# A hybrid RWKV-7 decoder on one core: raw fp32 products in the prologue, centring inside a transposition and split block sums in the scan

## The chip, the cores and the metric

The kernel runs on one core of one Trainium2 chip. The metric is the device time of one execution in microseconds (us), lower is better. TensorE (PE) does the matmuls, VectorE (DVE) and ScalarE (ACT) the element-wise work, GpSimd (POOL) a few memsets; SyncE (SP) and ScalarE issue the DMA transfers.

## What is computed

Two decoder layers of width 2048 on 272 positions (16 learned meta tokens and 256 tokens), all in fp32: RMS norm, RWKV-7 time mixing and a SwiGLU feed-forward, then stick-breaking attention and another feed-forward. The change touches the time mixing only:

```python
def _rwkv7_time_mix(h, ...):
    xx = _token_shift(h) - h
    xr, xw, xk, xv, xa, xg = (h + xx * mu[i] for i in range(6))
    r = xr @ w_r
    k = xk @ w_k
    v = xv @ w_v
    w = -softplus(-(dec_w0 + tanh(xw @ dec_w1) @ dec_w2)) - 0.5
    decay = exp(-exp(w))
    a = sigmoid(a_w0 + (xa @ a_w1) @ a_w2)
    g = sigmoid(xg @ g_w1) @ g_w2
    ...
    kk = heads(k * k_k)                     # 32 heads of 64
    kk = kk * rsqrt(maximum(sum(kk * kk, -1), 1e-24))
    k = k * (1.0 + (a - 1.0) * k_a)
    def step(state, inp):                   # over the 272 positions
        sa = einsum('bhvk,bhk->bhv', state, -kk_t)
        state = state * d_t + sa[..., None] * (kk_t * a_t) + v_t[..., None] * k_t
        return state, einsum('bhvk,bhk->bhv', state, r_t)
    _, y = lax.scan(step, s0, ...)
    y = (y - mean(y)) * rsqrt(var(y) + GN_EPS) * gn_w + gn_b
    bonus = sum(rh * kh * r_k, -1) * vh
    return ((y + bonus) * g) @ w_o
```

## The kernel before

Activations lie with channels on the partitions: 16 tiles of 128 channels by T = 272 positions. A product with a weight matrix is a sum of three fp32r matmuls of the high and low parts of both operands (`mm3k`, L187): `whi` is a rounding copy on ScalarE (L172), `wlo` the difference on VectorE (L173), and `hl` the pair of an activation (`split`, L250). A matmul on plain fp32 operands stands in the trace as two instructions, so each "x8" of such a row is four matmuls.

The time mixing has two stages. The **prologue** (L374) loads x on SP's queue (L385), squares it on ScalarE (L394), sums four squares each on VectorE (L398) and over partitions with a matmul of ones (`ss`, L399), makes the reciprocal root (`rstd_of`, `newton`), the normed `hn` (L452), and the mix `xi` for the keys (L429). The first G0 = 3 of 16 key blocks are multiplied together while x comes in (weights split by `presplit`, L407). `key_out` (L461) copies a finished block and adds its squares' head sums to `kq` (L469). The other 13 blocks follow one by one, and after each a generator `rest()` is stepped RSTEP times: it makes the LoRAs of decay and rate (`lr`, L497, raw fp32), the gate LoRA (mix 5 and `g_w1`, by `proj`), and the mixes for v and r. At the end `kq` becomes the inverse key norms `rk`, which are stored to DRAM (`rkd`) and loaded again as `rn` per pair of heads, spread over partitions.

The **scan** runs over 16 pairs of heads in chunks of 64 positions. `pair` (L580) is a generator; `interleave` (L546) starts a pair every STRIDE = 13 ticks and steps all open ones, so about three pairs overlap. Its steps, in order: `zw`, `za` (decay and rate), the projections of v and r (with `proj_steps`, which are the stream of split products that the small fp32 matmuls are set into), `vc` (values centred by a matmul with `cen`, which is the identity minus the head mean), `ba`/`bb` (scores, masked into G), `bonus` and `z0`, `b00`/`b01` (diagonal blocks, sent to DRAM, where 16-step triangular solves `Ts`, `Tt` are put together and come back), `yb`, `zb`, `tb`/`tv` (transpositions of keys and values), `kv`, `wa`, `rm0`/`rm1` (with `Ah`), `cb` (outputs and the state), `vb` (variance), `gp` (gate). PSUM banks come from three rings by name (FRONT, TAIL, the rest).

Within an engine, instructions run in a fixed order that a list scheduler with its own costs writes when the program is built; tile pools decide which buffer must be free first. SP's queue carries nearly all the weights. ScalarE's queue carries the transfers of the triangular solve.

Of the kernel before, what the change touches and what calls it, by code (L numbers as in the profile page):

```python
# [11 lines left out]
F32 = mybir.dt.float32  # L12
# [6 lines left out]
NK = D // 128  # L19
# [25 lines left out]
NSQ = 4  # L45
RSTEP = 7
KR = 8
# [13 lines left out]
def _consts():  # L61
# [14 lines left out]
    put("blk", blk)  # L76
    put("blk64", blk / 64)
# [6 lines left out]
    put("mask3", np.concatenate([incl, strict, incl], 1))  # L84
# [20 lines left out]
    first = pos  # L105
    put("onesD", np.full((128, 128), 1.0 / D))
# [17 lines left out]
class Builder:  # L124
# [141 lines left out]
    def build(self):  # L266
        tc, nc = self.tc, self.nc
        with ExitStack() as ctx:
# [6 lines left out]
            nc.scalar.dma_start(self.vecs, self.a["vecs"])  # L275
            self.dvec = {"hdw0": 0, "ha0": NK, "oka": 2 * NK}
            self.dvec.update({f"om{i}": (3 + i) * NK for i in range(6)})
            self.dv = cp.tile([128, 9 * NK + 4], F32, name="dv")
            b = 9 * NK
            nc.vector.memset(self.dv[:, b:b + 1], RMS_EPS)  # L280
            nc.vector.memset(self.dv[:, b + 1:b + 2], GN_EPS)
            nc.vector.memset(self.dv[:, b + 2:b + 3], 1.0)
            self.eps = self.dv[:, b:b + 1]
            self.gneps = self.dv[:, b + 1:b + 2]
            self.one = self.dv[:, b + 2:b + 3]

            def v16(name):
                i = VEC.index(name) * NK
                return self.vecs[:, i:i + NK]

            for dst, src in (("hdw0", "dec_w0"), ("ha0", "a_w0")):
                o = self.dvec[dst]
                nc.vector.tensor_scalar(self.dv[:, o:o + NK], v16(src), 0.5, None, ALU.mult)
            nc.vector.tensor_scalar(self.dv[:, 2 * NK:3 * NK], v16("k_a"), -1.0, 1.0,
                                    ALU.mult, ALU.add)
            nc.vector.tensor_scalar(self.dv[:, 3 * NK:9 * NK], self.vecs[:, 0:6 * NK], -1.0, 1.0,
                                    ALU.mult, ALU.add)
            nv = len(VEC) * NK
            self.kgain = self.vecs[:, nv:nv + 1]
            self.qgain = self.dv[:, b + 3:b + 4]  # L300
            nc.vector.tensor_scalar(self.qgain, self.vecs[:, nv + 1:nv + 2], 128.0 ** -0.5, None,
                                    ALU.mult)
# [34 lines left out]

    def time_mix(self):
# [4 lines left out]
        self.xs2 = self.hid_ctx.enter_context(tc.tile_pool(name="xs2", bufs=2 * NK))  # L343
        self.kp = self.hid_ctx.enter_context(tc.tile_pool(name="kp", bufs=NK))
# [6 lines left out]
        with ExitStack() as ctx:  # L351
            sp = ctx.enter_context(tc.tile_pool(name="sp", bufs=1))
            self.l2 = ctx.enter_context(tc.tile_pool(name="l2", bufs=2))
            self.dq = nc.scalar
            self.static = []
            self.s2 = []
            zero = sp.tile([128, 5, 65], F32, name="zero", tag="P")
            nc.gpsimd.memset(zero, 0.0)
            for i in range(2):
                st = {}  # L360
                for n, w in (("B0", 64), ("V0", 64), ("SC0", 128)):
                    st[n] = sp.tile([128, w], F32, name=f"{n}_{i}", tag=f"{n}_{i}")
                    nc.gpsimd.memset(st[n], 0.0)
                self.static.append(st)
                z = self.dram.tile([10, 65, 64], F32, name=f"s2_{i}", tag=f"s2_{i}", bufs=1)
                self.dq.dma_start(z.rearrange("s i t -> (s i t)").rearrange("(p x) -> p x", p=128),
                                  zero.rearrange("p a t -> p (a t)"))
                self.s2.append(z)
            self.interleave(lambda p: self.pair(p, sp), STRIDE, self.wo_head())
# [4 lines left out]
    def prologue(self, hid):  # L374
# [3 lines left out]
        with ExitStack() as ctx:  # L378
# [3 lines left out]
            hn = [self.xs2.tile([128, T + 1], F32, name="hn", tag="s") for _ in range(NK)]  # L382
            xx = [self.xs2.tile([128, T], F32, name="xx", tag="s") for _ in range(NK)]
            for k in range(NK):
                nc.sync.dma_start(xx[k], a["xT"][:, k, :])  # L385
# [14 lines left out]
            rstd = self.rstd_of(ss[:, :T])  # L400


            w0 = [[] for _ in range(G0)]
            raws = []
            n = 0

            def presplit(k0):  # L407
                nonlocal raws, n
                if k0 % 8 == 0:
                    raws = []  # L410
                    for m in range(G0):
                        raw = self.wraw.tile([128, 1024], F32, name="raw", tag="raw")
                        nc.sync.dma_start(raw, a["w_k"][m][:, k0 * 128:k0 * 128 + 1024])
                        raws.append(raw)
                for m in range(G0):
                    pool, t = (wx, ("w", "w")) if n < NWX // 2 else (self.whl, ("whi", "wlo"))
                    hi = pool.tile([128, 512], F32R, name="whi", tag=t[0])
                    lo = pool.tile([128, 512], F32R, name="wlo", tag=t[1])
                    n += 1
                    part = raws[m][:, k0 % 8 * 128:k0 % 8 * 128 + 512]  # L420
                    A.copy(hi, part)
                    V.tensor_tensor(lo, part, hi.bitcast(F32), ALU.subtract)
                    for k in range(4):
                        w0[m].append((hi[:, k * 128:k * 128 + 128], lo[:, k * 128:k * 128 + 128]))
# [5 lines left out]

            def mix(i, k, pool):
                x = pt.tile([128, T], F32, name="xi", tag="tmp")
                mixed(i, k, x)
                if pool is not self.xs2:
# [9 lines left out]
                  for m in range(G0)]  # L444
            xk = []
            for k in range(NK):
                if k % 4 == 0:
                    presplit(k)
                if k == 0:
                    nc.sync.dma_start(self.consts, a["consts"][:, :NC1])  # L450
                V.memset(hn[k][:, 0:1], 0.0)
                V.scalar_tensor_tensor(hn[k][:, 1:], xx[k], self.vec("g_mix0", k), rstd, ALU.mult,  # L452
                                       ALU.mult)
# [5 lines left out]
            self.k = []  # L459

            def key_out(m, ps):  # L461
# [4 lines left out]
                s2 = pt.tile([128, T], F32, name="s2", tag="tmp")  # L466
                A.activation(s2, kt, AF.Square, scale=self.vec("k_k", m))
                o, _ = CONST["sel"]
                nc.tensor.matmul(kq[:, :T], self.consts[:, o + 30 - 2 * m:o + 62 - 2 * m], s2,  # L469
                                 start=m == 0, stop=m == NK - 1)  # L470
# [16 lines left out]
            def rest():  # L487

                for i, name in ((1, "dec_w1"), (4, "a_w1")):
                    ps = self.psd.tile([128, 512], F32, name="lr", tag="sd")[:96, :T]  # L490
                    for k in range(NK):
                        if k % 4 == 0:
                            raw = wx.tile([128, 384], F32, name="raw", tag="w")
                            nc.sync.dma_start(raw, a[name][:, k * 96:k * 96 + 384])
                        x = self.xs1.tile([128, 2 * T], F32, name="xi", tag="hl")[:, :T]
                        mixed(i, k, x)
                        nc.tensor.matmul(ps, raw[:, k % 4 * 96:k % 4 * 96 + 96], x,  # L497
                                         start=k == 0, stop=k == NK - 1)
                        yield 1
                    t = pt.tile([128, T], F32, name=name, tag="tmp")[:96]  # L500
                    if i == 1:
                        A.activation(t, ps, AF.Tanh)
                        self.hw = hsplit(t, name)
                    else:
                        A.copy(t, ps)
                        self.ha = hsplit(t, name)
                for k in range(KR):
                    self.xr.append(mix(0, k, self.xs2))
                    yield 1
                x = []  # L510
                for k in range(NK):
                    x.append(mix(5, k, self.xs1))
                    yield 1
                for j in range(2):
                    ps = self.proj(a["g_w1"][j], x)
                    g = pt.tile([128, T], F32, name="hg", tag="tmp")
                    A.activation(g, ps, AF.Tanh, scale=0.5)
                    V.tensor_scalar(g, g, 0.5, 0.5, ALU.mult, ALU.add)
                    self.hg.append(hsplit(g, f"hg{j}"))
                    yield 1  # L520
# [3 lines left out]
                for k in range(KR, NK):  # L524
# [11 lines left out]
            self.rk = hid.tile([32, T], F32, name="rk")  # L536
# [664 lines left out]
```

## Time and profile before

| | us |
|---|---|
| median of 3 runs (lowest, highest) | 2740.06 (2737.32, 2741.23) |
| profiled execution, its time and its span | 2741.77, 2740.0 |
| first key matmul | 21.2 |
| first `zw` of the scan | 179.8 |
| last `zw` of the scan | 608.3 |
| granted TensorE clock over the span | 0.995 |

The profile is of one execution; its times are us from the start of the span. A row of the timeline is: start, duration, engine, line, operation, output<-inputs, shapes, count, and in brackets the idle time before it with what ended it. Matmuls overlap, so what one costs is the distance between two starts. A row of the chain of waits is start, duration and what ran.

### The profile page before, as it was taken

The numbers are of one execution on the slowest core, as the hardware profiler recorded it, in microseconds if no ns is written. First come the engines' busy times: TensorE is split into PE (matmuls) and PEld (weight loads), VectorE is DVE, ScalarE is ACT, GpSimd is POOL, SyncE is SP. The second block draws the span as 40 slices with busy tenths as digits, with TensorE's granted clock in tenths as the row PEclk, the third lists the DMA queues.
The fourth block names the chain that finished last, engine by engine and source line by source line (L and its number), as shares of the span: only waits on it lengthen the run. The fifth ranks groups of instructions, "written<-read, shape, count | busy, mean of one in ns | idle before, by whom it ended". The sixth has DMA issues, their size and how long they took to land.

```text
span 2740.0 us, 53870 instructions
## 1 busy us (share of the span) xinstructions
PE 2689.3 (98%) x20862; PEld 2475.0 (90%) x20862; DVE 1864.8 (68%) x4176; ACT 1493.5 (55%) x3005; POOL 1.2 (0%) x11
## 2 busy tenths in 40 slices
PE   6999999998999999999999999999999999999999
PEld 5888888887999999999999999988888888888888
DVE  7677788786666555555556876577776666666665
ACT  6774555555554444444445764477555455454553
POOL 0000000000000000000000000000000000000000
PEclk9999999999999999999999999999999999999999
DMA  5443333332655555555555555533555665665655
GB/s 169 135 152 100 104 96 103 104 95 83 210 173 168 181 177 167 185 176 162 187 176 167 180 164 169 169 119 105 189 187 179 196 188 180 197 189 179 199 177 179
DMA packets 181279, 439.50 MB, mean 160 GB/s; under 512 B 57984, under 2 KB 84000, under 8 KB 181024
## 3 DMA queue, kind: packets, MB, share of 16 engines
q1 hardware_dynamic: 137632, 428.56, 49.4%
q10 hardware_dynamic: 43392, 7.52, 1.5%
q8 instruction: 163, 2.67, 0.4%
q14 instruction: 92, 0.75, 0.1%
HBM read 430.27 MB, written 5.74 MB: 159 GB/s over the span
## 4 chain that ended last, share of the span: by engine, by line
PE 91%; DVE 3%; DMA 3%; ACT 2%; ACTq 1%; issue 0%; SPq 0%; DVEq 0%
PE mm L197 22%; PE mm L191 16%; PE mm L193 16%; PE mm L192 15%; PE mm L196 11%; DMA raw<-w_k 1%; PE cb L903 1%; PE yb L831 1%; PE rm L871 1%; PE zb L848 1%; PE hms L1038 1%; PE cb L896 1%; PE z L1115 1%; DVE G L721 0%; PE ba L715 0%
## 5 line engine op out<-in xcount | busy, mean ns | idle before, releaser
L173 DVE TENSOR_TENSOR wlo<-raw,whi 128x512 fp32r<-128x512 f32 (+1 forms) x1596 | 1079.0, 679 | 622.3 <-ACT whi L172 598.7
L172 ACT CAST whi<-raw 128x512 fp32r<-128x512 f32 (+1 forms) x1596 | 967.6, 611 | 906.2 <-PE mm L192 577.0
L191 PE MATMUL mm<-hl,whi 128*128 128x272 f32 x3424 | 996.9, 292 | 19.4 <-ACT hl L254 18.5
L193 PE MATMUL mm<-hl,wlo 128*128 128x272 f32 x3424 | 995.9, 291 | 0.0
L192 PE MATMUL mm<-hl,whi 128*128 128x272 f32 x3424 | 991.4, 290 | 0.4 <-DVE hl L255 0.3
L197 PE MATMUL mm<-hl,whi 128*128 128x512 f32 x2624 | 919.8, 395 | 0.0
L196 PE MATMUL mm<-hl,wlo 128*128 128x256 f32 x2624 | 740.6, 282 | 0.0
L191 PEld LDWEIGHTS mm<-hl,whi 128*128 128x128 f32 x3424 | 645.8, 189 | 27.7 <-ACT hl L254 20.5
L192 PEld LDWEIGHTS mm<-hl,whi 128*128 128x128 f32 x3424 | 652.6, 191 | 4.2 <-DVE hl L255 1.3
L193 PEld LDWEIGHTS mm<-hl,wlo 128*128 128x128 f32 x3424 | 647.9, 189 | 4.8 <-issue 1.8
L197 PEld LDWEIGHTS mm<-hl,whi 128*128 128x128 f32 x2624 | 492.5, 188 | 112.7
L196 PEld LDWEIGHTS mm<-hl,wlo 128*128 128x128 f32 x2624 | 494.3, 188 | 0.6
L213 DVE TENSOR_TENSOR h<-h,mm 128x256 f32<-128x256 f32 (+1 forms) x224 | 93.9, 420 | 6.6 <-PE mm L197 6.0
L206 ACT COPY c<-mm 128x256 f32<-128x256 f32 x104 | 38.8, 373 | 79.0 <-PE mm L197 78.9
L191 PE MATMUL mm<-hi,whi 128*128 128x272 f32 x256 | 79.3, 310 | 0.0
L192 PE MATMUL mm<-lo,whi 128*128 128x272 f32 x256 | 77.0, 301 | 0.0
L193 PE MATMUL mm<-hi,wlo 128*128 128x272 f32 x256 | 76.6, 299 | 0.0
L193 PEld LDWEIGHTS mm<-hi,wlo 128*128 128x128 f32 x256 | 48.8, 191 | 2.9 <-issue 2.4
L191 PEld LDWEIGHTS mm<-hi,whi 128*128 128x128 f32 x256 | 48.9, 191 | 2.4
L192 PEld LDWEIGHTS mm<-lo,whi 128*128 128x128 f32 x256 | 48.9, 191 | 1.0
L428 ACT ACTIVATE u<-hn,vecs 128x272 f32<-128x272 f32 x96 | 45.2, 515 | 4.8 <-DVE hn L452 4.8
L1009 ACT ACTIVATE s<-t 128x272 f32<-128x272 f32 (+1 forms) x88 | 37.5, 426 | 18.6 <-DVE t L208 18.5
(275 smaller groups left out, 2158.6 us busy)
## 6 DMA issues: line engine op xcount, KB each, us to landing
raw<-w_gate SPq DMA_DIRECT2D x176, 512.0 KB
raw<-w_up SPq DMA_DIRECT2D x176, 512.0 KB
raw<-w_down SPq DMA_DIRECT2D x128, 512.0 KB
raw<-w_down SPq DMA_DIRECT2D x128, 192.0 KB
raw<-w_k SPq DMA_DIRECT2D x32, 512.0 KB
raw<-w_v SPq DMA_DIRECT2D x32, 512.0 KB
raw<-w_r SPq DMA_DIRECT2D x32, 512.0 KB
raw<-w_o SPq DMA_DIRECT2D x32, 512.0 KB
```

Of the source, the lines that this page charges most:

```text
L172: nc.scalar.copy(hi, part)
L173: nc.vector.tensor_tensor(lo, part, hi.bitcast(F32), ALU.subtract)
L191: mm(out, w[0], x[0], start=first, stop=False)
L192: mm(out, w[0], x[1], start=False, stop=False)
L193: mm(out, w[1], x[0], start=False, stop=last)
L196: mm(out[:, :n], w[1], x[0], start=first, stop=False, skip_group_check=True)
L197: mm(out, w[0], x[2], start=False, stop=last, skip_group_check=True)
L206: self.nc.scalar.copy(c, out[:, n:])
L213: self.nc.vector.tensor_tensor(h, h, out[:, c:c + n], ALU.add)
L428: A.mul(u, hn[k][:, :T], self.vec(f"mu{i}", k))
L831: PE.matmul(yb[r, i * 64:i * 64 + 64], An[r, i], Tt[r, i], start=True, stop=True)
L1009: nc.scalar.activation(s[:, :n], t[:, :n], AF.Silu)
```

## The change

In the prologue:

- x is loaded on two queues, eight tiles on SP and eight on ScalarE; `vecs` and the constants too are on ScalarE's queue, and the first block of `w_k` is SP's second load. There are 3 buffers for squares instead of 4.
- The rstd chain is one VectorE op shorter: the sign and the factor one half go into the gain `mg0`.
- The three first key blocks are multiplied as raw fp32 (48 matmuls) and not as three split products each (144), so their weights aren't split.
- The gate LoRA is made as the other two LoRAs were, raw fp32 with one mix per channel tile, all three together; `rest()` is stepped 4 times a block and gives xv first, the LoRAs, then xr.
- `kq` is in two halves; the first eight blocks' key norms are stored when block 7 is done.

In the scan:

- `vc` goes. v itself is copied to V0 and ARV, and the centring is done where v is transposed: `z0` with `cen` in the place of the identity, `tv` as eight matmuls of 64 columns, against the identity or `cen`, in the place of four transpositions. The masks take two VectorE ops in the place of four.
- The block sums `bonus` and `vb` are two fp32r matmuls each (high and low part, `head_sums`) with an fp32r block matrix, in the place of one fp32 matmul.
- From VectorE to ScalarE go the copies of `pe`, the affines of `ta` and `k2`, the copy `Ah` and a square; memsets of P go to GpSimd.
- Two pools track reuse of their buffers per tile (`reuse_waits="tile"`).

```diff
-NSQ = 4
-RSTEP = 7
+NSQ = 3
+RSTEP = 4
...
+    def load_tokens(self):
+        for k in range(NK):
+            (nc.sync, nc.scalar)[k % 2].dma_start(self.xx[k], self.a["xT"][:, k, :])
+        nc.scalar.dma_start(self.vecs, self.a["vecs"])
...
-            rstd = self.rstd_of(ss[:, :T])
+            A.activation(r, ms, AF.Ln, bias=self.eps)
+            A.activation(r, r, AF.Exp, scale=-0.5)
+            V.tensor_tensor(rn, r, r, ALU.mult)
+            V.scalar_tensor_tensor(rn, ms, RMS_EPS, rn, ALU.add, ALU.mult)
+            V.scalar_tensor_tensor(rn, rn, -3.0, r, ALU.add, ALU.mult)
...
-                xk.append(mix(2, k, x0))
+                x = xtile()
+                mixed(2, k, x)
                 for m in range(G0):
-                    self.mm3k(ps[m][:, :T], w0[m][k], xk[k], k == 0, k == NK - 1)
-            kq = self.psc.tile([32, 512], F32, name="kq", tag="sc")
+                    o = k % 4 * 128
+                    nc.tensor.matmul(ps[m][:, :T], w0[m, k // 4][:, o:o + 128], x,
+                                     start=k == 0, stop=k == NK - 1)
+                xk.append(self.split(x, x0))
+            kq = [self.psc.tile([32, 512], F32, name="kq", tag="sc") for _ in range(2)]
...
+                if m % 8 < 7:
+                    return
+                ...
+                nc.sync.dma_start(self.rkd[2 * (m - 7):2 * (m + 1)], rk[:16])
...
+                    for i, n in names:        # (1, dec_w1), (4, a_w1), (5, g_w1 twice)
+                        x = xtile()
+                        mixed(i, k, x)
+                        c = 96 if i < 5 else 128
+                        for j in range(len(n)):
+                            nc.tensor.matmul(bk[i, j][:c, :T], w[i, j][:, k % 4 * c:k % 4 * c + c], x,
+                                             start=k == 0, stop=k == NK - 1)
+                    yield 1
...
+        def head_sums(out, block, x, hi):
+            lo = self.rstd_p.tile([128, T], F32R, name="lo", tag="rstdt")
+            V.tensor_tensor(lo, x, hi.bitcast(F32), ALU.subtract)
+            PE.matmul(out, block, hi, start=True, stop=False)
+            PE.matmul(out, block, lo, start=False, stop=True)
...
+        A.copy(V0[:, 32:32 + META], vp[:, :META])
+        A.copy(ARV[:, :, 2], vp[:, META:].rearrange("p (c t) -> p c t", t=C))
...
-        vc = bank("vc")
-        PE.matmul(vc[:, :T], self.cst("cen"), v, start=True, stop=True)
-        A.copy(V0[:, 32:32 + META], vc[:, :META])
-        A.copy(par(ARV, 2, 0), c4(vc[:, :T]))
...
-        PE.matmul(bp[:, :T], self.cst("blk"), rs, start=True, stop=True)
+        head_sums(bp[:, :T], self.blk[0], rs, high(rs))
...
-            PE.matmul(z0[h, 128:192], V0[h], self.cst("eye64")[h], start=True, stop=True)
+            PE.matmul(z0[h, 128:192], V0[h], self.cst("cen")[h, h], start=True, stop=True)
...
-                x = ARV[:, q * 2 + r, 1 - r:3 - r]
-                PE.transpose(tv[:, u:u + 128], x.rearrange("p s t -> p (s t)"), self.cst("ident"))
+                PE.matmul(tv[hs[r], u:u + 128], ARV[:, c, 1], self.cst("ident"), start=True, stop=True)
+                PE.matmul(tv[hs[1 - r], u:u + 128], ARV[:, c, 2], self.cst("cen"), start=True, stop=True)
...
-        V.tensor_copy(Ah, wa.rearrange("p (a s t) -> p a s t", a=4, s=2)[:, :, 0])
+        A.copy(Ah, wa.rearrange("p (a s t) -> p a s t", a=4, s=2)[:, :, 0])
...
-        PE.matmul(vb[:, :T], self.cst("blk64"), sq, start=True, stop=True)
+        head_sums(vb[:, :T], self.blk[1], sq, high(sq))
```

What the scheduler makes of it, at three places. **ScalarE at the start of the program.** A name in brackets is a semaphore waited for; DMAHW1, 3, 5, 7 count the landings of earlier transfers, of which DMAHW3's is the first block of `w_k` (`raw`). Before:

```order
L275 DMA vecs<-vecs 128x290
L387 ACT_TABLE_LOAD
L394 ACTIVATE sq<-xx 128x272 [waits DMAHW1_49]
L394 ACTIVATE sq<-xx 128x272 [waits DMAHW2_49]
L394 ACTIVATE sq<-xx 128x272 [waits DMAHW3_49]
L394 ACTIVATE sq<-xx 128x272 [waits DMAHW4_49]
```

and after:

```order
L317 DMA vecs<-vecs 128x290
L316 DMA xx<-xT 128x272
L413 ACT_TABLE_LOAD
L316 DMA xx<-xT 128x272 x2
L316 DMA xx<-xT 128x272 [waits DMAHW1_49]
L316 DMA xx<-xT 128x272 [waits DMAHW3_49]
L316 DMA xx<-xT 128x272 [waits DMAHW5_49]
L316 DMA xx<-xT 128x272 [waits DMAHW7_49]
L316 DMA xx<-xT 128x272 [waits DMAHW1_49]
L420 ACTIVATE sq<-xx 128x272
L420 ACTIVATE sq<-xx 128x272 [waits DMAHW2_49]
L420 ACTIVATE sq<-xx 128x272 [waits DMAHW4_49]
```

Behind the vecs come eight loads of x (`xx`), five of which wait for an earlier landing, and all stand ahead of the first square (`sq`).

**SP's queue from the last key blocks to the first pairs of the scan.** Before, `rkd` is the store of all the inverse key norms (`rk`), and the first `rn` loads them for pair 0; the `lora` rows are the second LoRA weights, `w_v` and `w_r` the projections of the first pairs. Before:

```order
L161 DMA raw<-w_v 128x1024 x2
L161 DMA raw<-w_r 128x1024 x2
L161 DMA raw<-w_v 128x1024 x2
L614 DMA w_2285<-lora 128x512
L161 DMA raw<-w_r 128x1024
L544 DMA rkd<-rk 32x272
L614 DMA w_2580<-lora 128x512
L161 DMA raw<-w_r 128x1024
L625 DMA rn<-rkd 128x1x272
```

After, in the key blocks,

```order
L541 DMA raw<-a_w 128x384
L160 DMA raw<-w_k 128x1024
L507 DMA rkd<-rk 16x272
L541 DMA raw<-g_w 128x512 x2
L160 DMA raw<-w_k 128x1024 x2
```

and, at the end of the key blocks,

```order
L160 DMA raw<-w_k 128x1024 x7
L160 DMA raw<-w_v 128x1024 x2
L160 DMA raw<-w_r 128x1024 x2
L160 DMA raw<-w_v 128x1024 x2
L657 DMA w_2032<-lora 128x512
L668 DMA rn<-rkd 128x1x272
L507 DMA rkd<-rk 16x272
L657 DMA w_2327<-lora 128x512
```

The store of the first half (pairs 0 to 7) has moved among the key weights, and pair 0's `rn` stands ahead of the store of the second half.

**TensorE in the scan, where values are transposed.** `mm` rows are the stream of split products, the others belong to two pairs under way. Before:

```order
L848 MATMUL zb<-Ys,Tn 64x64 x8
L801 MATMUL tv<-consts,ARV 128x128 x4
L191 MATMUL mm<-hi,whi 128x272
L192 MATMUL mm<-lo,whi 128x272
L857 MATMUL wa<-X,Tt 64x128 x8
L810 MATMUL kv<-X,G 64x64 x8
L695 MATMUL vc<-v,consts 128x272
L871 MATMUL rm_5811<-G,Ah 64x128 x2
L871 MATMUL rm_5812<-G,Ah 64x128 x2
```

After, from the last two of the eight `tv` matmuls on:

```order
L834 MATMUL tv<-consts,ARV 64x128
L835 MATMUL tv<-consts,ARV 64x128
L891 MATMUL wa<-X,Tt 64x128 x8
L844 MATMUL kv<-X,G 64x64 x8
L905 MATMUL rm_6078<-G,Ah 64x128 x4
L190 MATMUL mm<-hi,whi 128x272
L905 MATMUL rm_6079<-G,Ah 64x128 x4
L191 MATMUL mm<-lo,whi 128x272
L192 MATMUL mm<-hi,wlo 128x272
```

`vc` no longer stands between `kv` and the first `rm`, and one product now divides the two `rm` banks. In the same way `b00`, `b01` and `yb`, which were one block of small matmuls, stand at three places, with products between, and the low part of `bonus` stands inside `z0`. A pair has 16 such visits to small matmuls where it had 14.

More of the change, by code (lines that the diff above doesn't have):

```diff
@@ L105, in _consts @@
     first = pos
+    put("blk", blk)
     put("onesD", np.full((128, 128), 1.0 / D))
@@ L274, in build @@
             self.vecs = cp.tile([128, NV], F32, name="vecs")
[L275 to L302, printed above, removed]
+            self.dv = cp.tile([128, 12 * NK + 5], F32, name="dv")
             self.rstd_p = ctx.enter_context(tc.tile_pool(name="rstd", bufs=1))
@@ L366, in time_mix @@
                 self.dq.dma_start(z.rearrange("s i t -> (s i t)").rearrange("(p x) -> p x", p=128),
-                                  zero.rearrange("p a t -> p (a t)"))
+                                  zero)
                 self.s2.append(z)
+            o, n = CONST["blk"]
+            raw = sp.tile([128, 5, 64], F32, name="blk", tag="Tt", bufs=BUFS["Tt"])
+            raw = raw.rearrange("p c t -> p (c t)")[:, :n]
+            self.dq.dma_start(raw, a["consts"][:, o:o + n])
+            self.blk = []
+            for i, x in enumerate((1.0, 1.0 / HD)):
+                t = sp.tile([128, n], F32R, name="blk", tag=f"blk{i}")
+                nc.scalar.activation(t, raw, AF.Copy, scale=x)
+                self.blk.append(t)
             self.interleave(lambda p: self.pair(p, sp), STRIDE, self.wo_head())
@@ L381, in prologue @@
             pt = ctx.enter_context(tc.tile_pool(name="pt", bufs=3))
[L382 to L385, printed above, removed]
+            hn, xx = self.hn, self.xx
             self.pre0 = tc.keep_in_program_order(
@@ L399, in prologue @@
                 nc.tensor.matmul(ss[:, :T], od, acc, start=g == 0, stop=g == NK - 4)
-            rstd = self.rstd_of(ss[:, :T])
[L403 to L424, printed above, removed]
+            ms = ss[:, :T]
+            r = self.rstd_p.tile([128, T], F32, name="rstd", tag="rstd")
+            rn = self.rstd_p.tile([128, T], F32, name="rstdt", tag="rstdt")
+            A.activation(r, ms, AF.Ln, bias=self.eps)
[3 more added lines that the diff above has]
+            V.scalar_tensor_tensor(rn, rn, -3.0, r, ALU.add, ALU.mult)
             def mixed(i, k, out):
@@ L465, in key_out @@
                 self.k.append(kt)
[L466 removed]
+                s2 = xtile()
                 A.activation(s2, kt, AF.Square, scale=self.vec("k_k", m))
                 o, _ = CONST["sel"]
[L469 to L470 removed]
+                o += 30 - 2 * (m % 8)
+                nc.tensor.matmul(kq[m // 8][:, :T], self.consts[:, o:o + 32], s2,
+                                 start=m % 8 == 0, stop=m % 8 == 7)
+                if m % 8 < 7:
+                    return
+                rk = hid.tile([32, T], F32, name="rk", tag="rk")
+                t = self.rstd_p.tile([128, T], F32, name="kqs", tag="rstd")[:32]
+                V.tensor_scalar(t, kq[m // 8][:, :T], 1e-24, None, ALU.max)
+                t2 = self.rstd_p.tile([128, T], F32, name="kqr", tag="rstdt")[:32]
+                A.activation(rk, t, AF.Ln)
+                A.activation(rk, rk, AF.Exp, scale=-0.5)
+                self.newton(rk, t, 0.0, t2)
+                nc.sync.dma_start(self.rkd[2 * (m - 7):2 * (m + 1)], rk[:16])
             for m in range(G0):
@@ L487, in rest @@
             def rest():
[L489 to L520, printed above, removed]
                 for k in range(NK):
@@ L605, in bank, with high @@
             return self.psc.tile([128, 512], F32, name=name, tag="sc")
+        def head_sums(out, block, x, hi):
[3 more added lines that the diff above has]
+            PE.matmul(out, block, lo, start=False, stop=True)
+        def high(x):
+            hi = self.rstd_p.tile([128, T], F32R, name="hi", tag="rstd")
+            A.copy(hi, x)
+            return hi
         def c4(ap):
```

178 lines of the change are left out of this document (119 added, 59 removed).

## The prediction, made before the changed kernel ran

> **What bounds the kernel now.** I read the page first, then the waits of TensorE, then windows over the stages, then the timeline and the chain of waits at the places that the change touches.
>
> ```profile
> span 2740.0 us, 53870 instructions
> PE 2689.3 (98%) x20862; PEld 2475.0 (90%) x20862; DVE 1864.8 (68%) x4176; ACT 1493.5 (55%) x3005; POOL 1.2 (0%) x11
> ```
> ```profile
> PE mm L191 <- ACT hl L254: 18.5, 7, 6.7
> PE b L766 <- DVE bv L729: 5.8, 11, 0.6
> ```
> ```profile
> 21.20:53.40 32.20, 26.41 (x150) 24.16 (x150) 26.99 (x61) 21.21 (x50) 0.00 (x0) 0.90 0.44 138
> 53.40:179.80 126.40, 122.53 (x859) 108.28 (x858) 93.55 (x198) 100.88 (x230) 0.99 (x7) 1.00 0.45 145
> 190.00:195.00 5.00, 2.76 (x26) 2.38 (x26) 4.85 (x16) 0.62 (x1) 0.00 (x0) 0.89 0.37 135
> 195.00:200.00 5.00, 5.00 (x45) 3.80 (x44) 1.82 (x6) 1.44 (x5) 0.00 (x0) 0.77 0.72 228
> 225.00:230.00 5.00, 2.22 (x12) 1.67 (x11) 1.34 (x7) 1.69 (x4) 0.00 (x0) 0.80 0.25 53
> 230.00:235.00 5.00, 5.00 (x46) 4.34 (x45) 3.50 (x12) 0.83 (x2) 0.00 (x0) 0.51 0.33 96
> 300.00:500.00 200.00, 196.37 (x2391) 167.64 (x2390) 160.26 (x577) 115.46 (x277) 0.00 (x0) 1.00 0.36 101
> ```
>
> In the second fence each row gives a waiting instruction, what it waited for, total us, times, longest. In the third it is the stretch and its length, then busy us of PE, PEld, DVE, ACT and POOL, the granted clock, DMA share and GB/s. TensorE is busy 98% of the span, so outside a few waits only its own work counts. The scan (300 to 500) leaves it idle 3.6 of 200 us. VectorE and ScalarE, from which much work is taken, are filled to 80% and 58% there, and what they give back is free time, apart from TensorE's wait for `bv`: 5.8 us in 11 times, 0.53 a pair. The waits that can be won lie in the first 53 us and in the fill of the pipeline (190 to 235), and there an idle is paid twice: the windows behind the two holes run at clocks of 0.77 and 0.51. From the projection `w_o` on, neither the work nor its order changes, so the last 2000 us are costed at nothing.
>
> **The start: x on two queues.**
>
> ```profile
> 3.50 0.97 ACT L394 ACTIVATE sq<-xx 128x272 f32<-128x272 f32 x2 [1.02 <-DMA xx<-xT]
> 12.27 0.43 ACT L394 ACTIVATE sq<-xx 128x272 f32<-128x272 f32 x1 [0.73 <-PE ss L399]
> 13.23 1.28 PE L399 MATMUL ss<-sq,od 128*128 128x272 f32 x2 [1.00 <-DVE sq L398]
> 17.38 0.69 DVE L422 TENSOR_TENSOR wlo<-raw,whi 128x512 fp32r<-128x512 f32 x1 [0.29 <-ACT whi L421]
> 18.79 0.51 DVE L452 SCALAR_TENSOR_TENSOR hn<-xx,vecs,rstd 128x272 f32<-128x272 f32 x1
> 21.23 1.05 PE L191 MATMUL mm<-hl,whi 128*128 128x272 f32 x3 [6.72 <-ACT hl L254]
> ```
> ```profile
> 4.96 0.43 SPq L385
> 8.76 7.95 DMA raw<-w_k
> ```
> ```profile
> 63.64 4.36 DMA raw<-w_k
> ```
>
> Before, ScalarE squares from 3.50, and the last square (12.27) waits not for data but for a `ss` matmul to free a buffer. Afterwards ScalarE's own queue holds vecs and eight x loads (0.43 each) ahead of the first square, and the fifth of them waits until a block of `w_k`, now SP's second load, has landed. Such a block takes between 4.36 us (row at 63.64) and 7.95 us (row at 8.76), so that one issued at 1.2 lands at 5.6 to 9.2. I take 6.5, near the low end, as one x tile and not sixteen is ahead of it in its queue. Four issues more put the first square at about 8.0, 4.5 us later. Three square buffers instead of four I cost at nothing, because the pace is already that of the sums; uncovered, each group of four would wait one `ss` matmul, 1.28 us. With the same 9.7 us from first square to last `ss` matmul, that one starts at 17.7 against 13.23. From there to the first key matmul it is 8.0 us before. The splits of weights among the VectorE steps go (the 0.69 at 17.38 and another ahead of the first split of x), so do one op of the rstd chain and the split of x ahead of the matmul; behind `hn` stand only u and xi, three steps of about 0.5. I take 5.6. The key matmuls start at 23.3 instead of 21.2: **+2.1**, between −2.4 (no wait in the queue) and +4.8 (7.95 holds).
>
> The Trainium skill (DMA: Bandwidth & Descriptors, Issuing engines are not separate DMA queues) says that transfers started from several engines run on the same 16 DMA engines, and only the issuing time is saved. The trace agrees as far as it goes, since the issuing (0.43 a tile) isn't what the last square waits for; by that rule alone this part would be worth nothing rather than +2.1.
>
> **Three key blocks raw.**
>
> ```profile
> 60.73 0.29 PE L193 MATMUL mm<-hl,wlo 128*128 128x272 f32 x1
> 60.85 2.00 PE L497 MATMUL lr<-xi,raw 128*96 128x272 f32 x8
> 62.78 0.65 PE L469 MATMUL kq<-s,consts 128*32 128x272 f32 x2
> ```
>
> A split product starts 0.12 us after the one before; eight fp32 passes, which are four fp32 matmuls, take 1.93 us, 0.24 a pass. 144 products (18 us) become 48 raw matmuls (96 passes, 23.0 us). The stretch from 21.2 to 53.4 is 32.2 us long though, TensorE idle for 5.8 of it and at a clock of 0.90: it waits for `hl` and weight splits. Twelve pairs of weight splits go, x is split only for later blocks, and the loads of the second half no longer wait for a buffer. So the stage becomes TensorE's: 23.0, plus 2.6 lost to the clock (0.10 of 32.2 is 3.2 before, some of it behind later holes), plus 1.0 where VectorE doesn't keep up: 26.6 to the first key sum, **−5.6**. The cover there is thin: VectorE needs hn, xi and a split per k, three steps of 0.4 to 0.5, against six passes, 1.44. If it falls behind throughout, 2 us more go.
>
> The Trainium skill (TensorE: Matmul & The Clock Gate, Part 1: The HAM clock gate) puts the slow time at about 3.4 us of activity. At half pace that loses 1.7 us; the 3.2 us that this stretch lost is more, and the holes in it are why I don't go lower. By the page the stage would come out 0.9 us shorter.
>
> **Gate LoRA raw.** Its 96 split products (11.8 us) become 32 raw matmuls (64 passes, 15.4): +3.6. In the stretch from 53.4 to 179.8 TensorE idles 3.9 us, and with fewer splits for VectorE and ScalarE I take 2.1 of that back: **+1.5** (between −0.3 and +3.6). The LoRAs' new places and the smaller step of the generator only reorder work on a TensorE that is full. The pipeline's first `zw` (179.8 now) comes 2.0 us earlier.
>
> **The fill.**
>
> ```profile
> 183.45 6.67 DMA rn<-rkd
> 192.84 0.37 PE ba L715
> 222.34 6.27 DMA Tt<-s
> ```
>
> The chain of waits goes from the last key block through `rk`, its store and its load (6.67 us) to `ba` of pair 0, for which TensorE idles 2.24 us (190 to 195) and then loses 0.11 and 0.23 of 5 us each to the clock, 1.7: 3.9. With `kq` in two halves the first half's store stands ahead of all of that on SP's queue, and pair 0's `rn` waits for eight key blocks only. What is late next is the triangular solve of pair 0: `Tt` returns from DRAM at 228.6, an idle of 2.78 us (225 to 230), and the clock costs 1.0 and 2.45 more: 6.2. Its chain has the same links but starts with `rn`; I take a third, 2.1, and keep 0 and 6.2 as bounds. **−6.0**.
>
> **The scan, per pair.**
>
> ```profile
> 437.73 0.66 PE L801 MATMUL tv<-consts,ARV 128*128 128x128 f32 x4
> 438.14 0.37 PE L191 MATMUL mm<-hi,whi 128*128 128x272 f32 x1
> ...
> 439.68 0.73 PE L695 MATMUL vc<-v,consts 128*128 128x272 f32 x2
> 440.33 1.30 PE L871 MATMUL rm<-G,Ah 64*64 64x128 f32 x16
> ```
> ```profile
> 438.00 0.40 ACT L661 COPY v<-mm 128x272 f32<-128x272 f32 x1
> 438.42 0.59 ACT L802 COPY X<-tv 128x512 f32<-128x512 f32 x1
> ```
> ```profile
> 439.70 0.43 DVE L861 COPY Ah<-wa 128x256 f32<-128x256 f32 x1
> ```
> ```profile
> 449.36 0.29 PE L192 MATMUL mm<-hl,whi 128*128 128x272 f32 x1
> 449.58 0.33 PE L903 MATMUL cb<-Rh,S 64*64 64x64 f32 x4
> ...
> 450.07 0.29 PE L191 MATMUL mm<-hl,whi 128*128 128x272 f32 x1
> ...
> 450.44 0.69 PE L916 MATMUL vb<-sq,consts 128*128 128x272 f32 x2
> ...
> 451.18 0.37 PE L715 MATMUL ba<-ARV,BK 64*128 64x128 f32 x1
> ...
> 453.62 0.69 PE L727 MATMUL bonus<-rs,consts 128*128 128x272 f32 x2
> 454.24 0.30 PE L734 MATMUL z<-AR,B 64*64 64x32 f32 x4
> ```
>
> Starts are what counts. `vc` occupies 0.65 (439.68 to 440.33) and goes: −0.65. `bonus` occupies 0.62; two split products take 0.25, but the second stands inside `z0` and cuts it in two. A visit from the stream of split products to small fp32 matmuls costs about 0.3 by itself: 0.71 from 449.36 to 450.07, less two products and some 0.16 of small passes. So bonus is −0.07. `vb` with the `gp` product behind it occupies 0.74, afterwards three products, 0.38: −0.36. `tv` was 0.41 for four transpositions; eight matmuls of half the columns, if two of them run side by side, are sixteen passes of 128 columns in eight slots, about twice the work and a switch: +0.55. `b00`, `b01` and `yb`, one visit now, become three: +0.6. In exchange `b00` waits only for ScalarE's copy and `b01` for `bv`, with split products between: −0.53, the wait in the fence of waits. `Ah` moves to ScalarE, queued there behind the copies of X (0.59), v (0.40) and V0, and `rm0` needs it at once; `vc` had filled that gap of 0.65. I take half of it: +0.35. Other moves of copies and affines from VectorE to ScalarE are hidden under TensorE's 98%; if ScalarE were late, the whole pair stands behind it. The sum is −0.1 a pair, **−1.6** over 16. Ends: −0.45 a pair (no wait for `Ah`), −7; +0.95 (`rm0` waits for all three copies, 1.42), +15. At the tail the chain to the last output changes a copy of 0.4 for a shorter rstd: 0.
>
> **The sum.** +2.1 − 5.6 + 1.5 − 6.0 − 1.6 = −9.6. The profiled execution took 2741.77 (span 2740.0 and 1.8 around it), 1.7 above the median of 2740.06; 2741.77 − 9.6 is 2732.2, on the median's scale 2730.5, so **2731**.
>
> **Rivals.**
> - ScalarE's queue becomes what TensorE waits for in the scan: `rm0` stands until X, v and `Ah` are copied, 1.42 a pair. At +0.95 a pair the scan gains 15 us, against −8.0 before it: 2747. It ends as slower from +0.85 a pair on, and eats the gain from +0.5. For it: TensorE has no slack there, and the filler `vc` is gone; `tv` at two slots for one (+0.5 to +0.8) would do the same. Against it: ScalarE is filled to only 58%. Chance 0.22.
> - The early gain is taken by the next wait: `Tt` comes as late as before and idles longer, the squares start at 10.7. Then −9.6 + 2.7 + 2.1 + 1 of clock: −3.8, 2736, no measurable change. For it: each hole shown is followed by another one in the chain. Chance 0.25.
> - The whole of it works: squares hardly delayed (−2), `Tt`'s hole closed too (−4), the scan at −0.45 a pair (−5): 2719. For it: holes cost double by the clock, and each closed one returns that. Chance 0.13.
> - My forecast, 2722 to 2735: chance 0.40.
>
> Under 0.2% (5.5 us) the measurement of this kernel can't tell a difference from none. Faster: nearly all of the forecast and the third rival, 0.50; within: 0.27, the second rival and the forecast's edge; slower: 0.23. The range reaches from 2715 (the third rival, with its clock regained too) to 2749 (the first, 2 beyond its price).
>
> **What would show it.** First square near 8 and key matmuls near 23; the first `kq` near 50; no hole ahead of the first `ba`, one of about 2 us ahead of `yb`; no wait for `bv` in the scan, and successive pairs as far apart as now, to 0.2 us. I'm wrong if the pairs stand over 0.5 us further apart, if `rm0` shows a wait for `Ah` of over half a us a pair, or if ScalarE's squares start at 4 or past 10.

## The result, and the profile after

The changed kernel takes 2750.32 us (median of 5 runs, 2748.74 to 2752.61) against 2738.69 for the kernel before on the same chip (5 runs): 1.0042 times as long, 95% interval 1.0028 to 1.0057. It is slower by about 11.6 us; the prediction was 2731, and its range ended at 2749. Of the two profiled executions the one before took 2741.77 and the one after 2748.74, so that the traces show 7.0 us of the 11.6 between them; the rest is the spread of runs.

First the marks that the prediction named. The start, in the timeline of the changed kernel:

```profile
1.69 6.92 ACTq L316 DMA_DIRECT2D xx<-xT  x7
8.65 0.75 ACT L420 ACTIVATE sq<-xx 128x272 f32<-128x272 f32 x2 [5.71 <-DMA xx<-xT]
...
18.69 1.27 PE L425 MATMUL ss<-sq,od 128*128 128x272 f32 x2 [1.54 <-DVE sq L424]
24.21 6.09 PE L477 MATMUL mm<-xi,raw 128*128 128x272 f32 x13 [4.24 <-DVE xi L439]
```

ScalarE is busy with issuing x until 8.6, and squares from 8.65 (3.50 before). The key matmuls start at 24.2 (21.2 before). Windows of the changed kernel, columns as in the prediction: the raw key blocks, the other key blocks, the two stretches that held the holes of the fill, and eight pairs of the steady scan. Behind them, in a second fence, the same eight pairs before.

```profile
24.20:51.30 27.10, 25.63 (x98) 20.38 (x98) 23.01 (x53) 18.67 (x45) 0.00 (x0) 1.00 0.35 116
51.30:181.30 130.00, 125.69 (x832) 109.41 (x832) 82.87 (x176) 92.08 (x206) 1.06 (x9) 1.00 0.44 139
190.00:195.00 5.00, 4.64 (x66) 3.53 (x65) 4.38 (x10) 3.31 (x8) 0.14 (x2) 1.00 0.55 161
225.00:230.00 5.00, 5.00 (x75) 4.25 (x74) 4.86 (x20) 3.21 (x8) 0.00 (x0) 1.00 0.06 18
344.40:583.40 239.00, 237.70 (x2883) 203.95 (x2884) 175.29 (x602) 151.33 (x384) 1.09 (x16) 1.00 0.35 99
```
```profile
344.20:577.30 233.10, 228.96 (x2804) 195.47 (x2801) 187.64 (x681) 133.52 (x321) 0.00 (x0) 1.00 0.36 102
```

The holes ahead of `ba` and `yb` are gone but for 0.36 us, and with them the half pace: the clock is 1.00 in both stretches. But a steady pair takes 239.0/8 = 29.87 us instead of 29.14. Per pair TensorE idles 0.16 us instead of 0.52, and is busy 1.09 longer (237.70 against 228.96, over eight). VectorE got 12 us lighter over these pairs and ScalarE 18 heavier; neither decides anything here. Three of the waits of TensorE in the changed kernel (us in total, times, longest) show that `bv` has left the list and little has come in its place.

```profile
PE yb L865 <- DMA Tt<-s: 1.9, 2, 1.5
PE bonus L642 <- DVE G L755: 1.4, 4, 0.4
...
PE rm L905 <- ACT Ah L895: 0.4, 1, 0.4
```

What the busy time is made of. From the starts of all matmuls of those eight pairs I summed the distance from each start to the next by the tile written; us per pair:

| tile | before | after | |
|---|---|---|---|
| vc | 0.66 | 0 | −0.66 |
| tv | 0.41 | 1.02 | +0.61 |
| wa, kv, rm | 2.34 | 2.74 | +0.41 |
| bonus | 0.62 | 0.48 | −0.15 |
| vb, gp | 1.47 | 1.12 | −0.35 |
| z0 | 0.50 | 0.74 | +0.25 |
| b00 and b01 | 0.29 | 0.77 | +0.48 |
| mm (before it holds the wait of 0.52 ahead of b) | 14.75 | 14.85 | +0.10 |

The remaining tiles make +0.04. The step from a product into a visit to small matmuls stands in the row of the product (mm), the step out of it in the row of its last small pass. In the timeline of TensorE the cuts can be seen (`b` is b00 in one row and b01 in the other):

```profile
381.89 0.98 PE L891 MATMUL wa<-X,Tt 64*64 64x128 f32 x14
382.65 0.27 PE L844 MATMUL kv<-X,G 64*64 64x64 f32 x2
...
383.45 0.66 PE L905 MATMUL rm<-G,Ah 64*64 64x128 f32 x8
...
394.77 0.28 PE L770 MATMUL z<-consts,V 64*64 64x64 f32 x2
394.98 0.39 PE L643 MATMUL bonus<-lo,blk 128*128 128x272 f32 x1
395.30 0.32 PE L770 MATMUL z<-consts,V 64*64 64x64 f32 x2
...
397.26 0.46 PE L798 MATMUL b<-BK,ARV 64*64 64x64 f32 x8
400.34 0.46 PE L798 MATMUL b<-BK,ARV 64*64 64x64 f32 x8
```

In the timeline before, one row held all sixteen b passes:

```profile
458.53 0.48 PE L766 MATMUL b<-BK,ARV 64*64 64x64 f32 x16 [0.52 <-DVE bv L729]
```

Start to end that took 0.48, behind the wait for `bv`; now two rows of eight take 0.46 each, three us apart.

### The profile page after: what moved, and what is told of

Its sections match the earlier page's. It is cut to its first block, busy times and chain, and to the rows that moved or that the text cites. A ratio compares the mean times of both kernels' runs of the same rounds, so it can differ in the third digit from the quotient of the medians.

```text
span 2747.0 us, 54045 instructions
## 1 busy us (share of the span) xinstructions
PE 2702.8 (98%) x20942; PEld 2483.8 (90%) x20942; DVE 1826.2 (66%) x3988; ACT 1515.9 (55%) x3101; POOL 3.3 (0%) x43
## 4 chain that ended last, share of the span: by engine, by line
PE 95%; DMA 2%; DVE 1%; ACT 1%; issue 0%; ACTq 0%; DVEq 0%; SPq 0%
PE mm L196 22%; PE mm L190 16%; PE mm L192 16%; PE mm L191 16%; PE mm L195 11%; PE lr L547 1%; PE yb L865 1%; DMA raw<-w_k 1%; PE cb L937 1%; PE rm L905 1%; PE zb L882 1%; PE hms L1074 1%; PE wa L891 1%; PE cb L930 1%; PE z L1151 1%; PE mm L477 0%
## 5 line engine op out<-in xcount | busy, mean ns | idle before, releaser
L190 PE MATMUL mm<-hl,whi 128*128 128x272 f32 x3344 | 972.6, 291 | 8.4 <-ACT hl L253 5.6
L192 PE MATMUL mm<-hl,wlo 128*128 128x272 f32 x3344 | 969.7, 290 | 0.0
L191 PE MATMUL mm<-hl,whi 128*128 128x272 f32 x3344 | 967.8, 289 | 0.0
L190 PEld LDWEIGHTS mm<-hl,whi 128*128 128x128 f32 x3344 | 629.8, 188 | 16.2 <-ACT hl L253 5.9
L191 PEld LDWEIGHTS mm<-hl,whi 128*128 128x128 f32 x3344 | 636.0, 190 | 3.0 <-issue 0.5
L192 PEld LDWEIGHTS mm<-hl,wlo 128*128 128x128 f32 x3344 | 630.5, 189 | 3.6 <-issue 1.5
L196 PEld LDWEIGHTS mm<-hl,whi 128*128 128x128 f32 x2624 | 492.5, 188 | 111.5
L195 PEld LDWEIGHTS mm<-hl,wlo 128*128 128x128 f32 x2624 | 493.9, 188 | 0.6
```

The source lines that it names most:

```text
L190: mm(out, w[0], x[0], start=first, stop=False)
L191: mm(out, w[0], x[1], start=False, stop=False)
L192: mm(out, w[1], x[0], start=False, stop=last)
L195: mm(out[:, :n], w[1], x[0], start=first, stop=False, skip_group_check=True)
L196: mm(out, w[0], x[2], start=False, stop=last, skip_group_check=True)
```

## Experiments

Theory A: the change is slower because the order that comes with it cuts the small matmuls of a pair into more and less overlapping pieces, and because ScalarE's queue holds up the start; the new prologue by itself gains. Rival B: the new operations (`tv`, the split sums) are dearer in themselves. Rival C: ScalarE's copies are what TensorE waits for. In all texts "visit" is an entry from the stream of split products into small fp32 matmuls. Every ratio is against the kernel before on the same chip. The changed kernel's own interval, 1.0028 to 1.0057, overlaps those of experiments 2, 3, 4 and 5, so that between these and it the windows decide and not the times. A pass is one of the two instructions of an fp32 matmul.

**1 and 2. The scan of before; x on SP's queue.** The first takes back the whole `pair` generator, the second one line.

```diff
-            (nc.sync, nc.scalar)[k % 2].dma_start(self.xx[k], ...)
+            nc.sync.dma_start(self.xx[k], ...)
```

> The changed prologue with the pair generator of before (vc, four transpositions, single fp32 block sums, Ah on VectorE). Theory A (the scan as it is ordered now costs TensorE 0.7 us a pair more): pairs again 29.1 us apart, first zw near 181.4 as in the changed kernel, the fill keeps its gain; 2733 to 2738 us. Rival B (the prologue costs it): pairs matter little, the time stays above 2745.

> All sixteen x loads back on SP's queue, everything else as changed. Theory A (the squares wait for ScalarE's own issues): first square near 3.5 instead of 8.65, key matmuls near 20.5 instead of 24.2, first zw 3 to 4 us earlier, 2747 us. Rival (x is limited by the transfers themselves, the queue doesn't matter): key matmuls at 23.5 or later, no change of the time.

Experiment 1: 2738.32 us, ratio 0.9996 (0.9986 to 1.0006). Its first `zw` comes at 181.8, its sixth at 310.5, its last at 603.4; its pairs are 29.1 apart. So the scan carries the slowdown. What prologue and fill gained together stays inside the noise of the runs; in the trace the last `zw` is 4.9 us ahead of before, where the prediction had 8.0. Experiment 2: 2746.62, ratio 1.0029 (1.0017 to 1.0040). Its timeline:

```profile
3.54 0.43 ACT L420 ACTIVATE sq<-xx 128x272 f32<-128x272 f32 x1 [1.08 <-DMA xx<-xT]
...
16.54 0.49 ACT L430 ACTIVATE rstd<-ss,dv 128x272 f32<-128x272 f32 x1 [2.07 <-PE ss L425]
```
```profile
20.74 9.59 PE L477 MATMUL mm<-xi,raw 128*128 128x272 f32 x29 [4.24 <-DMA raw<-w_k]
```

Squares from 3.54 and key matmuls from 20.7, as expected: the second queue cost 3.5 us at this place, of which 2.5 are left at the first `zw` (178.9 against 181.4; 3 to 4 were expected). The key matmuls now wait last for a block of `w_k`, which stands behind all of x on SP's queue.

**3, 4 and 6. Order only.** The matmuls of `z0` are pinned behind the low product of `bonus` (3); also `yb` begins with the half that lands last (4); or those of `b00` and `b01` are chained in turn (6).

```diff
+            self.tc.keep_in_program_order(   # each z0 matmul (3, 4)
             PE.matmul(z0[h, 0:32], B0[h], ...)
-                for r in hs:                 # first yb (4)
+                for r in hs[::-1]:
+            if n: self.tc.keep_in_program_order(mm)   # b00, b01 (6)
```

> Order only: z0's six matmuls are kept together behind the low product of bonus, so bonus no longer cuts z0 in two; the order has 15 visits to small fp32 matmuls a pair instead of 16. Theory A (each visit costs about 0.35 by itself): pairs 29.5 us apart instead of 29.86, 2745 us. Rival C (what costs is the new work, or waits for ScalarE's copies, wherever it stands): 29.8 to 29.9, or a new wait for lo ahead of z0.

> Order only: as the one before, and yb begins with the half whose transfer is issued last, so that it isn't begun alone; the scheduler then makes an order with 10 to 11 visits a pair instead of 16. Theory A: 0.35 for each visit, so pairs about 27.9 us apart, 2722 us, if no new wait comes up. Rival C: visits are free, the pairs stay at 29.5 to 29.9, 2745 to 2750.

> Order only: the matmuls of b00 and b01 (two row halves of the array, two banks) alternate again but for the first. Theory A (apart, each half has the array alone, and the sixteen passes cost 0.77 where alternating they cost 0.29): b down to about 0.4, pairs 29.5 us apart, 2745 to 2746. Rival: the second bank comes free late, so the chain of b waits and the pairs stay at 29.9.

Medians and ratios: (3) 2745.48, 1.0027 (1.0017 to 1.0036); (4) 2758.85, 1.0071 (1.0054 to 1.0088); (6) 2741.71, 1.0008 (0.9998 to 1.0017). The windows over eight pairs, of 3, then 4, then 6:

```profile
342.80:580.40 237.60, 234.61 (x2883) 201.92 (x2883) 175.24 (x601) 151.22 (x384) 1.10 (x16) 1.00 0.35 100
```
```profile
343.00:591.60 248.60, 231.44 (x2886) 202.17 (x2884) 171.79 (x601) 153.54 (x384) 1.10 (x16) 0.99 0.33 95
```
```profile
342.00:580.00 238.00, 236.70 (x2883) 202.94 (x2882) 175.11 (x601) 151.23 (x384) 1.09 (x16) 1.00 0.34 100
```

(3) went as A said in sign and time: TensorE's busy time fell by 0.39 a pair, of which 0.2 was lost again to b's bank, so a pair took 29.70, not 29.5. (4) missed: the busy time did fall, to 28.93 a pair, but TensorE now idled 2.1 a pair. In (6) a pair gained 0.11 and not the expected 0.36 (29.75), since the first of the eight matmuls of b still stands alone, three us ahead of the other seven:

```profile
394.67 0.32 PE L798 MATMUL b<-BK,ARV 64*64 64x64 f32 x2
...
397.74 0.47 PE L798 MATMUL b<-BK,ARV 64*64 64x64 f32 x14
```

From start to start b fell from 0.77 to 0.65 a pair. So the overlap that came back is worth 0.12, and most of what b costs more than before stays as long as there are two visits. The time came out 3 us below the expected 2745, which A doesn't explain: of the 7.3 us of span, 2.8 came from the first zw to the sixth and 3.9 behind the last one, which no theory named. What (4) waited for, in its waits, in ScalarE's timeline and, third, in the chain of waits:

```profile
PE bonus L642 <- ACT hi L647: 11.1, 8, 3.1
```
```profile
457.72 0.49 ACT L955 ACTIVATE rs<-vb,dv 128x272 f32<-128x272 f32 x1
460.19 1.30 ACTq L818 DMA_DIRECT2D Tt<-s  x2
461.53 1.28 ACT L956 ACT_TABLE_LOAD   x1 [3.32 <-issue]
462.82 0.43 ACT L956 ACTIVATE rs<-rs 128x272 f32<-128x272 f32 x1
```
```profile
455.90 4.27 DMA s<-Ts
```

ScalarE does nothing from 458.2 to 461.5: its next entry is the load of `Tt`, which waits for the store that goes before it (`s<-Ts`, 4.27 us). The copy of bonus's high part stands behind that and a table load.

**5. The block sums as one fp32 matmul each again.**

```diff
-        head_sums(bp[:, :T], self.blk[0], rs, high(rs))
+        PE.matmul(bp[:, :T], self.blk[0], rs, start=True, stop=True)
```

> The changed kernel with bonus and vb as one plain fp32 matmul each, as before; the scheduler's order then has 14 visits a pair and z0 whole, b00 and b01 still apart. Theory A (a visit costs 0.35, the split sums themselves save TensorE about 0.5 a pair): +0.5 for the sums, -0.35 for z0, -0.35 for another visit less, pairs 29.6 to 29.7 us apart, 2747. Rival B (the split sums are what makes a pair dearer): pairs 29.2 or less, 2740.

2754.55, ratio 1.0052 (1.0039 to 1.0066). Both missed: pairs are dearer still, 31.2, of which 1.4 is idle. Rival B falls for the sums. For `tv` no run tests it; there the table has its price, +0.61. The waits name the reason for the idle, b's bank (freed by the copy `BV`), 0.9 each time, and `Tt`:

```profile
PE b L798 <- ACT BV L775: 9.0, 10, 1.3
...
PE yb L865 <- DMA Tt<-s: 3.3, 6, 1.1
```

**7 and 8. The prologue alone, without the second queue; and with the gate LoRA in split products.** 7 is 1 and 2 together; 8 puts back all of `rest()` as before, with its order of mixes and its 7 steps a block.

> Scan of before, changed prologue, all x on SP's queue: the first two experiments together. Theory A (their effects add): key matmuls at 20.7, first zw near 179, pairs 29.1, 2735 us, faster than before by 0.2%. Rival: the earlier start meets weights that have not landed, and 2738 stays.

> As e7, and the gate LoRA as split products again (with the order of the other LoRAs as before). Theory A (raw costs TensorE 3.6 us there and frees no wait): first zw 2 to 3.5 us earlier than in e7, 2732 us. Rival (the splits of mix 5 and g_w1 keep VectorE and ScalarE from the key blocks): no earlier zw, 2735 or more.

7: 2733.40, ratio 0.9979 (0.9970 to 0.9987), faster than both kernels; first `zw` at 177.3, 2.5 ahead of before. 8: 2735.72, 0.9988 (0.9978 to 0.9997). Its first `zw` comes at 175.3, 2.0 earlier than in 7, as A said, but its fourth at 255.7 against 248.5. The holes of the fill are back: from the first `zw` to the sixth TensorE idles 7.2 us at a clock of 0.96, as before. So the time is where the rival had it. Since one edit changed both, the run can't tell which part of the new `rest()` keeps the fill closed. The intervals of 7 and 8 overlap, so which is the better isn't shown.

**9 and 10. The pins together; b apart in the old scan.** 9 is 2, 3 and 6 together. 10 writes the four matmuls of b00 (eight passes) ahead of the four of b01 in experiment 7's kernel, within the same visit:

```diff
-        for c, h in order:
+        for c, h in sorted(order, key=lambda x: x[1]):
```

> The changed kernel with x on SP's queue and the two pins on the order (z0 whole, b00 and b01 alternating). Theory A (the effects add: 3.7 + 4.8 + 8.6 less than the changed kernel): pairs 29.5 to 29.6 us apart, 2734 us. Rival (the pins change the tail or the fill by chance, not the pairs): the sum doesn't come out, 2738 to 2742.

> The scan of before (as e7) with b00's matmuls written ahead of b01's; the order of all else is the same, 14 visits, both behind the wait for bv. Theory A (alternating matmuls of two row halves share the array): b from 0.28 to 0.5 or more a pair, pairs from 29.10 to 29.35 us apart, 2737 us. Rival (what cost in the changed kernel was the second visit alone): b stays at 0.28 to 0.35, 2733 us.

9: 2737.16, 0.9992 (0.9984 to 1.0001). The pairs came out at 29.6, the time 3 us above the sum: the 8.6 of experiment 6 did not add. 10: 2733.80, 0.9979 (0.9970 to 0.9988), pairs of 29.13, b at 0.28 from start to start as in 7.

```profile
450.51 0.48 PE L797 MATMUL b<-BK,ARV 64*64 64x64 f32 x16 [0.53 <-DVE bv L760]
```

A missed here, and the rival was met: the turn of the matmuls within a visit doesn't matter, so what b costs in the changed kernel comes with its second visit.

**11 and 12. The split sums in the old scan; Ah back on VectorE.**

```diff
-        PE.matmul(bp[:, :T], self.blk[0], rs, start=True, stop=True)   # 11, and vb alike
+        head_sums(bp[:, :T], self.blk[0], rs, high(rs))
-        A.copy(Ah, wa...)                                              # 12
+        V.tensor_copy(Ah, wa...)
```

> The scan of before (as e7) with bonus and vb as two split products each, the scheduler then makes an order of 13 to 15 visits. Theory A (the products save 0.35 with vb and 0.15 with bonus, the order they bring decides the rest): pairs 28.6 to 29.6 us apart, with waits for the high part's copy or for b's banks named in the trace; about 2731. Rival B (split sums are a loss by themselves): over 29.6.

> The changed kernel with the copy Ah on VectorE again; the scheduler makes an order of 13 to 16 visits. As predicted blind: rm0's wait for Ah goes, 0.2 to 0.35 a pair less, and fewer visits give another 0.5: pairs 29.2, 2742. Rival (ScalarE's queue in general, not this copy): no less than 29.7, with other waits for ScalarE.

11: 2756.06, 1.0064 (1.0053 to 1.0076), pairs of 31.0, of which 1.3 idle; TensorE is busy 29.7 where it was 28.6 in 7. A missed. The number is rival B's, but the rows of the sums themselves fell against 7 (`vb` with `gp` −0.24, bonus −0.05), while b rose from 0.28 to 0.65. 12: 2760.34, 1.0075 (1.0062 to 1.0088), pairs of 30.9, 1.0 idle. A missed in 12; the rival's bound (no less than 29.7) held, but it hadn't named the size: taking away a wait that stands in the list with 0.4 us cost 10 us, since the order became another one, whose longest waits in the scan are these five:

```profile
PE zb L882 <- DVE Ys L876: 3.1, 4, 1.1
PE bonus L642 <- ACT hi L647: 2.9, 4, 1.2
PE b L798 <- ACT BV L775: 2.7, 3, 1.0
PE yb L865 <- DMA Tt<-s: 2.2, 2, 1.6
PE b L798 <- DVE bv L762: 2.1, 2, 1.8
```

**13 and 14. The high part's copy on VectorE**, in 9's kernel and in 4's (both with x on SP).

```diff
-            A.copy(hi, x)
+            V.tensor_copy(hi, x)
```

> As e9 (new scan, x on SP, z0 whole, b chained), with the copy of the high part of bonus and vb on VectorE instead of ScalarE; the scheduler's order then has 12 visits a pair, the same every pair. Theory D (a visit between split products costs TensorE 0.3, provided the order holds no new wait): three visits fewer and b overlapped once more, 0.9 to 1.3 less than e9's 29.6: pairs 28.3 to 28.7 us apart, 2717 to 2722 us. Rival E (an order with fewer visits packs work that then waits, as in e4 and e12): idle of 0.8 or more a pair, pairs 29.3 or more, 2735 or slower.

> As e4 (z0 and yb whole, which waited 1.3 a pair for the high part's copy of bonus on ScalarE, behind the transfer of the triangular solve), with that copy on VectorE and x on SP; the order has 9 to 13 visits, not the same every pair. Theory E1 (the wait in e4 is for ScalarE's queue): no wait for hi left, idle below 0.6 a pair, pairs 29.0 or less, 2735 or less. Rival E2 (the wait is for rs, which comes late on VectorE, or for the buffer that bonus and vb share): the wait for hi stays at 0.8 or more a pair, above 2745.

13: 2738.48, 1.0000 (0.9990 to 1.0010). 14: 2730.56, 0.9971 (0.9960 to 0.9982): 8 us below before and the fastest by its median, though its interval overlaps those of 7 and 10. Windows over eight pairs, 13, then 14 (whose order differs from pair to pair):

```profile
341.70:576.10 234.40, 229.21 (x2881) 199.52 (x2880) 176.81 (x617) 146.61 (x369) 1.09 (x16) 1.00 0.35 101
```
```profile
337.50:567.40 229.90, 228.19 (x2897) 199.24 (x2897) 175.42 (x616) 145.69 (x368) 1.09 (x16) 1.00 0.36 103
```

14 against 4 bears out theory E1: with the copy off ScalarE's queue, the 11.1 us of waits for it shrink to one of 0.4, and the idle falls from 2.1 to 0.2 a pair, at 28.5 busy. The order became another one too (12 visits a pair, 10 in 4), so the copy isn't the only difference. 13 has nearly the same low busy time, 28.65, and 0.65 idle (b's bank, `Tt`). There D was right on the busy time; E's pairs (29.3 or more) and time (2735 or slower) were met, its idle (0.8 or more) nearly.

## Why the prediction was wrong

- **The scan, −0.1 a pair: this step failed.** It measured +0.73 in the steady pairs. `vc` (−0.65), `vb` with `gp` (−0.36) and `tv` (+0.55) came out near their prices, −0.66, −0.35 and +0.61. The term that was mis-sized is the one for the cut pieces. I set +0.6 for b00, b01 and yb in three visits against −0.53 for the wait, and −0.07 for bonus with z0's cut in it. The wait did go, and a visit cost what I had priced: the step into it takes 0.22 from start to start where products follow each other by 0.125, the step out of it 0.15 where small passes follow by some 0.02, and the product behind it 0.23, together 0.32 more. But b grew by 0.48 in its own row. Two steps out of a visit are about 0.27 of that; the other 0.2 is overlap of the two halves that is lost, for which I had set nothing (the profile before held the number, sixteen passes in one row of 0.48). In bonus and z0 the cut cost more than the split sum saved: −0.15 and +0.25, and 0.17 in the row mm, where the products ahead of them now take 0.21 and 0.22. Experiment 3 shows this part by itself, 0.39 of busy time a pair. And the product between the two `rm` banks is a further visit that I had not priced.
- **Ah on ScalarE, +0.35**: the place measured +0.41 over wa, kv and rm, but hardly as the wait that I named. `rm` has one wait of 0.4 in the list; the rest is that kv starts later within wa than before and overlaps with less of it. So the size came out by luck, and the product that now divides `rm` comes on top, 0.2 in the row mm. The ScalarE rival, which ended near the measured time (2747), is therefore not what happened.
- **The start, +2.1**: +3.0. The cause was right, as experiment 2 shows; the squares began at 8.65, not 8.0, and the last `ss` came 1.0 later than I set. By the rule of the Trainium skill that I had set against this part (DMA: Bandwidth & Descriptors, Issuing engines are not separate DMA queues) the second queue can save issuing time only; the runs agree that it brought nothing, and show a cost of 3.5 us that this section of the Trainium skill doesn't speak of. From `ss` to the key matmuls it was 5.5 (5.6 forecast).
- **Raw key blocks, −5.6**: from 24.2 to the first `kq` at 51.35 it is 27.1 (26.6 forecast), −5.1. Right, and so are its main parts: the first 13 passes take 6.09 us and start 0.45 apart, the later ones 0.23, which makes 2.9 lost to a slow start (2.6 forecast, 1.7 as the lower figure). The column of the granted clock says 1.00 there and doesn't show it. The 1.0 for VectorE came as a wait of 1.46 for ScalarE's copy `kt`.
- **Gate LoRA, +1.5**: 130.0 against 126.4, +3.6. The matmuls cost what was worked out; the 2.1 us of idle that I took back weren't there (4.3 us idle in this stretch after, 3.9 before). In experiment 8 the undone part brought 2.0 at the first `zw`. Start, key blocks and gate LoRA together missed by 3.5 there, +1.5 for −2.0.
- **The fill, −6.0**: with the old scan (experiment 1) first to sixth `zw` took 128.6 us against 135.3, −6.7, and the clock stayed at 1.00. The windows, before and in experiment 1:

```profile
179.82:315.13 135.31, 128.12 (x1395) 111.17 (x1395) 100.89 (x362) 70.13 (x170) 0.00 (x0) 0.96 0.38 109
181.84:310.46 128.62, 126.17 (x1396) 108.60 (x1394) 100.81 (x362) 69.94 (x173) 0.00 (x0) 1.00 0.39 114
```

The size of the fill was right, but not its parts. The second hole closed altogether and not by a third; idle fell by 4.7 us. For the clock behind the two holes I had priced 1.7 and 3.45 us, but TensorE's busy time over as many matmuls fell by only 2.0, and why by no more stays open. That the two errors cancel is luck. In the changed kernel the fill took 133.7, since the five pairs in it are dearer too and 22 more products of the stream fall into it.

As sum for the traces: +1.5 at the first `zw`, −1.6 to the sixth, +5.7 to the last, +1.3 behind it, together 7.0. What the 1.3 behind the last `zw` is, set at 0 in the prediction, stays open. What decides which order the scheduler makes of a small edit wasn't studied; that such an order, and not the edit, set the time in 5, 11 and 12 rests on their lists of waits, not on a run that held the order fixed.

## What to carry to other kernels

When the bounding engine is full, an edit there is priced by the order it leads to: count every visit to small matmuls, also where a product merely divides a group, and what overlaps inside them, and look for the copy that sits in an in-order queue behind a transfer. Loads that are put on a computing engine's queue delay that engine's first work by their waits, not only by their issuing (here seven issues of about 0.45 us took 6.92, and the first square came at 8.65 us, 3.54 without them). A closed hole in a pipeline's fill is worth its idle time and some of the half pace behind it, here 4.7 and 2.0 us.

## What the runs showed that I had not expected

Matmuls of the two row halves of the array overlap even if all eight passes of one half are issued ahead of the other's eight (0.28 us for both, experiment 10, as in turn); in two visits, with split products between, the same work takes 0.77, the steps out of the visits included. And one copy moved between engines (experiment 12) made the kernel 10 us slower, although it removed a wait.
